# Requesting modulation weights two blocks in front of their sums in a two-layer hybrid trunk

## The chip, the cores and the metric

The kernel runs on one core of one Trainium2 chip. The metric is the device time of one execution in microseconds; the time quoted for a kernel is the median of its runs. The core's engines are called by the profile's names: PE (TensorE, matrix products), DVE (VectorE), ACT (ScalarE), POOL (GpSimd) and SP (SyncE, which here only issues transfers).

## The reference

Two layers run one after the other over x, 1024 positions by 1024 columns in float32. Each layer is conditioned by a vector c: three rows of 1024 numbers (shift, scale and gate) come from one product of SiLU(c) with a matrix of 1024 by 3072.

```python
c_act = jax.nn.silu(c)
...
mod = c_act @ w_mod + b_mod
shift, scale, gate = jnp.split(mod[:, None, :], 3, axis=-1)
h = rms_norm(x, pre_gain) * (1.0 + scale) + shift
proj = h @ w_in
...
y = jnp.concatenate([a_out, r_out, g_out], axis=-1) @ w_out
return x + gate * rms_norm(y, post_gain)
```

Between proj and y three groups of heads work on slices of proj: softmax attention over a window of 128 positions, retention, and gated linear attention (GLA), each multiplied by a SiLU gate of its own. The shift and the scale of a layer are needed before its input projection; its gate is needed only at its very end.

## The kernel before

**Tiling.** The positions are eight tiles of 128, the 1024 input columns eight blocks k of 128 (KT = 8). The big products run in float32 split into a high and a low part, in three passes on PE. The weights are cut into units of 256 columns (named gg, rg, rq, rk, rv, gqk, gv, kv, aq0, aq1, ag0, ag1 and o0 to o3). A unit comes in four transfers (`load`, its `issue` and `conv`): each lands in a staging tile, ACT (L157) or DVE (L159) copies the high part out of it into a large array, arena, and DVE or POOL subtracts to get the low part (L577).

**Staging tiles.** `stage()` gives a tile st of 128 by 512 floats. There are five of them (BST = 5), used in turn; a transfer into a tile waits until the last reader of what lay there before is done. Weight quarters, modulation weights and two small rows of gains all go through these five. The loader of the weights has up to three quarters in flight (LAG = 2).

**The modulation sums.** `mod_third(l, j)` computes one third of mod for layer l: j = 0 shift, 1 scale, 2 gate. A third is two halves (hh) of 512 columns, and a half is eight blocks k. Its inner `part(hh, k)` takes a staging tile and asks for the block's 128 by 512 numbers of w_mod (the transfer "lwm"). DVE multiplies each tile by the column k of c_act and adds it to the accumulator acc (L389 for the first block where j < 2, L391 for all others). At the end of a half PE sums acc over the partitions. The first layer's shift and scale are computed by another path, with tiles wm. So four thirds run through this code: the gate of layer 0, then scale and shift of layer 1, both begun in layer 0, and the gate of layer 1. Each has 16 tiles, 64 in all.

**What sets the order.** The program is written as generators, the jobs: a planner keeps a clock (`clk`) that counts PE's work, and `pump()` resumes each job when its planned delay (`yield lat("mod2", l)`, from the table L: 4.8 us in layer 0, 4.0 us in layer 1) is over. PE's instructions then run in just the order in which they were written. On DVE, ACT, POOL and SP a scheduler orders the instructions, with its own estimates, from the dependences and the order of writing. All transfers into staging tiles are issued by SP, one after the other; while SP waits for a tile to come free, everything behind it in its queue waits too.

In the kernel before, `mod_third` keeps a list `wts` of requested tiles: a block's sum takes the tile requested one block earlier, and the next block's request goes out in the same step. So at most two of the five staging tiles hold w_mod: the one being summed and the next.

**Names in the rows.** acc is the accumulator of a third; mx, t, sm, gs and mid are work tiles of the branches (gs a GLA tile of decay factors); smx holds attention weights; aux and mm are accumulators of PE; mixS, srS, sgS and aoS are arrays in the chip's memory through which branch outputs pass and come back. L1370 and L1380 are a GLA chunk's products, L1242 and L1246 the norm of a retention or GLA output, L1185 the softmax's reciprocal, L1073 a step of the rotation.

Of the kernel before, what the change touches and what calls it, by code (L numbers as in the profile page):

```python
# [23 lines left out]
KT = D // P  # L24
# [69 lines left out]
def trunk(ctx: ExitStack, tc: tile.TileContext, ins, cst, out):  # L94
# [21 lines left out]
    def nm(s):  # L116
        uid[0] += 1
        return f"{s}_{uid[0]}"
# [7 lines left out]
    def stage():  # L126
        return gp.tile([P, 512], F32, tag="st", name=nm("st"), bufs=BST)
# [7 lines left out]
    def aux(dt=F32):  # L135
        return ps.tile([P, 512], dt, tag="aux", name=nm("aux"), bufs=8 - MMB)
# [24 lines left out]
    def dma(k, dst, src):  # L161
        i = {"S": nc.sync, "A": A, "P": G}[EN[k]].dma_start(dst, src)
        if k in ("ssg", "ssr", "lsr", "lsg", "smh"):
            mark[2] = i
# [10 lines left out]
    def mult(dst, lhsT, rhs, start, stop, cost=None):  # L175
        T.matmul(dst, lhsT, rhs, start=start, stop=stop)  # L176
        if cost is not None:
            clk[0] += cost
            return
        n = 1  # L180
        for d in rhs.shape[1:]:
            n *= d
        c = n / 2400.0
        if rhs.dtype == F32R:
            c = max(c, 0.107 if lhsT.shape[-1] > 64 else 0.055)
        else:
            c = max(4 * c, 0.21 if n > 2 else 0.03)
        clk[0] += c
# [5 lines left out]
    def lat(key, l):  # L194

        return L[key + "@1"] if l and key + "@1" in L else L[key]
# [4 lines left out]
    def flag(name, lat=0.0):  # L201
        flags[name] = clk[0] + lat
# [100 lines left out]
    def mod_rows(l, j, eng=nc.sync):  # L303
        rows = t1()[0:16, 0:P]
        eng.dma_start(rows[0:8, :], b_mod[l:l + 1, j * D:(j + 1) * D].rearrange("o (k p) -> (o k) p", p=P))
        eng.dma_start(rows[8:16, :], pre_g[l:l + 1, :].rearrange("o (k p) -> (o k) p", p=P))
        return rows

    def mod_rows_t(rows, pool=aux):
        pr = pool()  # L310
        transp(pr[:, 0:16], rows, ident[0:16, 0:16])
        rc = small(16)
        V.tensor_copy(rc, pr[:, 0:16])
        return rc

    def mod_cols(l, j, hh, pm, rc):
        res = modc[(l, j)]
        ks = slice(4 * hh, 4 * hh + 4)
        if j == 0:
            V.tensor_tensor(res[:, ks], pm[:, 0:4], rc[:, ks], ALU.add)  # L320
        else:
            col = small(4)
            V.tensor_tensor(col, pm[:, 0:4], rc[:, ks], ALU.add)
            V.scalar_tensor_tensor(res[:, ks], col, 1.0, rc[:, 8 + 4 * hh:12 + 4 * hh], ALU.add, ALU.mult)

    def mod_tile(l, j):
        modc[(l, j)] = cp.tile([P, KT], F32, name=nm(f"mod{j}"), tag=f"mod{j}")
# [27 lines left out]
    def mod_third(l, j):  # L355
        wv = w_mod[l].rearrange("(p k) n -> p k n", k=KT)
        if j < 2:
            mod_tile(l, j)
            rows = mod_rows(l, j)
            yield lat("mod1", l)  # L360
            rc = mod_rows_t(rows)
        else:
            res = cp.tile([P, D], F32, name=nm("modg"), tag="modg")
            modg[l] = res
        wts = []

        def part(hh, k):
            wt = stage()
            c0 = j * D + 512 * hh
            dma("lwm", wt, wv[:, k, c0:c0 + 512])  # L370
            return wt

        for hh in range(2):
            c0 = j * D + 512 * hh
            acc = gp.tile([P, 512], F32, tag="acc", name=nm("acc"), bufs=1)
            if j == 2:
                G.memset(acc, 0.0)
                nc.sync.dma_start(acc[0:1, :], b_mod[l:l + 1, c0:c0 + 512])
            for k in range(KT):
                if wts:  # L380
                    wt = wts.pop()
                else:
                    wt = part(hh, k)
                    yield lat("mod2", l)
                n = KT * hh + k + 1
                if n < 2 * KT:
                    wts.append(part(n // KT, n % KT))
                if k == 0 and j < 2:
                    V.tensor_scalar(acc, wt, c_act[:, k:k + 1], None, ALU.mult)  # L389
                else:  # L390
                    V.scalar_tensor_tensor(acc, wt, c_act[:, k:k + 1], acc, ALU.mult, ALU.add)  # L391
                if k < KT - 1:
                    yield lat("mod2", l)
            yield lat("mod3", l)
            pm = aux()
            if j < 2:
                for b in range(4):
                    mult(pm[:, b:b + 1], acc[:, b * P:(b + 1) * P], ones[:, 0:1], True, True)
                mod_cols(l, j, hh, pm, rc)
                if j == 0:  # L400
                    flag(("modh", l, hh), lat("mod4", l))
            else:
                mult(pm, allones, acc, True, True)
                gain = stage()
                nc.sync.dma_start(gain, post_g[l:l + 1, 512 * hh:512 * hh + 512].to_broadcast((P, 512)))
                V.tensor_tensor(res[:, 512 * hh:512 * hh + 512], pm, gain, ALU.mult)
            yield lat("mod5", l)
        flag(("mod", l, j), lat("mod6", l))

    def mod_all(l, js, after=None):  # L410
        if after is not None:
            yield (0.0, after)
        else:
            yield L["ms"]
        for j in js:
            yield from mod_third(l, j)
# [1641 lines left out]
```

## Time and profile before

| | us |
|---|---|
| median of 3 runs | 986.1 |
| lowest and highest run | 984.17, 991.72 |
| the profiled execution | 981.63 |
| its span, first to last instruction | 979.9 |
| mean granted clock of PE (share of full) | 0.985 |

The profile covers one execution, 4.5 us quicker than the median. Its span is what the timeline's times count from. In the profile's rows, busy time is counted for each engine alone; an engine's idle time stands in brackets ahead of the instruction that ended it, with the one it waited for. A clock below 1.00 in a slice means that PE was granted only part of its clock there. The transfers' view lists 64 requests of w_mod tiles and 96 of w_in tiles, 256 KB each.

### The profile page before, as it was taken

The page shows a single profiled execution, that of the slowest core. Times are in us where ns is not written, and L with a number is a line of the kernel's source. Part 1 is how long each engine was busy: PE and PEld are TensorE (multiplying, and loading weights), DVE is VectorE, ACT ScalarE, POOL GpSimd, SP SyncE. Part 2 cuts the span into 40 slices and gives each one's busy share as a digit, 9 for nine tenths or more (in the row PEclk, how much of TensorE's full clock was granted, in tenths as well). Part 3 has the DMA queues.
Part 4 walks back from the last instruction along what each step waited for, and adds up shares of the span by engine and source line. Part 5 has one row for each costly group of instructions (what it writes and reads, how often), then busy time and mean ns, then how long its engine had stood idle before and what let it go on. Part 6 is the DMA issues. An engine that isn't in the chain of part 4 may idle for free.

```text
span 979.9 us, 19345 instructions
## 1 busy us (share of the span) xinstructions
PE 953.8 (97%) x7133; PEld 833.6 (85%) x7133; DVE 676.6 (69%) x1627; ACT 409.8 (42%) x1121; POOL 216.6 (22%) x252
## 2 busy tenths in 40 slices
PE   6999999999999999999999999999999999999996
PEld 1799999889998877778889999998899887778885
DVE  3897768567766777746577497775556578665885
ACT  3875134323322565534455431133323258752431
POOL 1112001213220333331023010122232124550300
PEclk8999999989999999999999999999999999999999
DMA  9825324433145355777555583362133323379973
GB/s 317 305 73 175 122 77 122 138 120 120 56 131 152 100 169 152 218 217 266 181 172 180 191 262 111 109 194 80 45 94 109 105 57 112 116 207 290 306 253 125
DMA packets 133454, 155.04 MB, mean 158 GB/s; under 512 B 13760, under 2 KB 95468, under 8 KB 133360
## 3 DMA queue, kind: packets, MB, share of 16 engines
q1 hardware_dynamic: 128240, 145.30, 47.6%
q10 hardware_dynamic: 5120, 8.51, 2.3%
q8 instruction: 56, 0.92, 0.4%
q14 instruction: 38, 0.31, 0.1%
HBM read 111.30 MB, written 40.37 MB: 155 GB/s over the span
## 4 chain that ended last, share of the span: by engine, by line
PE 82%; DVE 7%; DMA 5%; ACT 3%; issue 2%; POOL 1%; SPq 1%; DVEq 0%; POOLq 0%; ACTq 0%
PE mm L176 62%; PE aux L176 16%; PE aux L191 4%; DMA wm<-in_w_mod_dram 2%; DMA st<-in_w_in_dram 1%; POOL sm L725 1%; DMA st<-in_w_mod_dram 1%; ACT t L781 1%; DVE arena L577 0%; DVE t L1371 0%; DVE sm L1242 0%; DMA mixS<-t 0%; DVE acc L391 0%; DVE mx L1380 0%; DMA su<-in_w_out_dram 0%
## 5 line engine op out<-in xcount | busy, mean ns | idle before, releaser
L176 PE MATMUL mm<-arena,arena 128*128 128x256 f32 (+2 forms) x2880 | 458.2, 315 | 1.1 <-DVE t L1267 0.9
L176 PEld LDWEIGHTS mm<-arena,arena 128*128 128x128 f32 x2880 | 398.8, 189 | 35.4 <-issue 2.1
L176 PE MATMUL mm<-arena,mx 128*128 128x512 f32 (+1 forms) x564 | 127.6, 383 | 0.0
L176 PE MATMUL mm<-arena 128*128 128x256 f32 (+2 forms) x768 | 126.9, 320 | 0.5 <-ACT arena L792 0.5
L176 PEld LDWEIGHTS mm<-arena 128*128 128x128 f32 x768 | 110.8, 195 | 12.0 <-issue 2.2
L176 PEld LDWEIGHTS mm<-arena,mx 128*128 128x128 f32 x564 | 101.9, 188 | 20.6 <-issue 0.4
L725 POOL TENSOR_TENSOR sm<-sm,mhalf 128x1 f32<-128x1 f32 (+1 forms) x48 | 49.4, 1031 | 265.8 <-DVE sm L724 256.3
L157 ACT ACTIVATE arena<-st 128x512 fp32r<-128x512 f32 x102 | 61.1, 627 | 62.3 <-DMA st<-in_w_in_dram 24.4
L577 POOL TENSOR_TENSOR arena<-st,arena 128x512 fp32r<-128x512 f32 x26 | 39.2, 1507 | 127.1 <-ACT arena L157 116.9
L157 ACT ACTIVATE t<-aux 128x512 f32<-128x512 f32 (+1 forms) x86 | 48.0, 593 | 44.7 <-PE aux L191 25.6
L577 DVE TENSOR_TENSOR arena<-st,arena 128x512 fp32r<-128x512 f32 x82 | 63.2, 790 | 2.9 <-ACT arena L157 1.7
L1186 POOL TENSOR_TENSOR smx<-smx,sm 128x512 f32<-128x512 f32 x32 | 35.2, 1099 | 134.1 <-DVE sm L1185 123.4
L1182 ACT ACTIVATE smx<-smx,sm 128x129 f32<-128x129 f32 x128 | 49.9, 393 | 14.5 <-DVE sm L1179 14.2
L391 DVE SCALAR_TENSOR_TENSOR acc<-st,c_act,acc 128x512 f32<-128x512 f32 x60 | 45.8, 763 | 11.3 <-DMA st<-in_w_mod_dram 10.7
L176 PEld LDWEIGHTS aux<-t,mx 32*128 32x128 f32 (+1 forms) x896 | 44.4, 195 | 7.2 <-issue 3.0
L176 PE MATMUL aux<-t,mx 32*128 32x32 f32 (+1 forms) x896 | 45.6, 280 | 3.0 <-DVE gs L1350 1.5
L781 ACT ACTIVATE t<-aux,mod,mod 128x128 f32<-128x128 f32 x72 | 27.2, 464 | 35.3 <-DVE t L1540 22.5
L157 ACT ACTIVATE t<-mm 128x256 f32<-128x256 f32 x40 | 15.0, 382 | 57.8 <-PE mm L176 57.7
L191 PE MATMUL aux<-c_ident,t 128*128 128x128 f32 (+1 forms) x228 | 34.4, 278 | 0.5 <-DVE t L1247 0.4
L1175 DVE COPY_PREDICATED smx<-c_curmask,aux 128x256 f32<-128x256 int32 x64 | 25.2, 447 | 9.5 <-ACT smx L157 8.3
L191 PEld LDWEIGHTS aux<-c_ident,t 128*128 128x128 f32 (+1 forms) x228 | 26.8, 143 | 5.6 <-issue 1.6
L1240 ACT ACTIVATE t<-aux 128x512 f32<-128x512 f32 x16 | 9.5, 595 | 51.0 <-PE aux L176 51.0
(240 smaller groups left out, 1380.5 us busy)
## 6 DMA issues: line engine op xcount, KB each, us to landing
st<-in_w_in_dram SPq DMA_DIRECT2D x96, 256.0 KB, 3.4
st<-in_w_mod_dram SPq DMA_DIRECT2D x64, 256.0 KB, 3.0
mixS<-t SPq DMA_DIRECT2D x48, 256.0 KB, 2.3
mx<-mixS SPq DMA_DIRECT2D x20, 512.0 KB, 5.8
st<-in_w_out_dram SPq DMA_DIRECT2D x28, 256.0 KB, 3.0
wm<-in_w_mod_dram SPq DMA_DIRECT2D x10, 512.0 KB, 5.0
t<-tabS SPq DMA_DIRECT2D x16, 256.0 KB, 2.6
aoS<-t SPq DMA_DIRECT2D x32, 128.0 KB, 4.1
```

Source lines behind the costliest of these rows:

```text
L157: A.activation(dst, src, AF.Copy)
L176: T.matmul(dst, lhsT, rhs, start=start, stop=stop)
L191: T.transpose(dst, src, idn)
L391: V.scalar_tensor_tensor(acc, wt, c_act[:, k:k + 1], acc, ALU.mult, ALU.add)
L577: e.tensor_tensor(lo, st, f(hi), ALU.subtract)
L725: G.tensor_tensor(r, r, mhalf[:, :w], ALU.pow)
L781: A.activation(hf[0][:, ks], x[:, ks], AF.Identity, scale=gain, bias=shift)
L1175: V.copy_predicated(sv, curmask.unsqueeze(1).to_broadcast((P, 2, P)), pv[:, :, n // P - 1, :])
L1182: A.activation(sm[:, h, :], sm[:, h, :], AF.Exp, bias=mx[:, h:h + 1], accum_out=sums[:, h:h + 1])
L1186: eng("pn").tensor_tensor(sm[:, :, 0:128], sm[:, :, 0:128], rs.unsqueeze(2).to_broadcast((P, 4, P)), ALU.mult)
L1240: A.activation(sq, po, AF.Square)
```

## The change

Only the loop over the blocks in `mod_third` changes. A third now requests its first two tiles at once before its first delay; each block takes the oldest requested tile and asks for the tile two blocks further on. So three of the five staging tiles hold w_mod while a third runs: one being summed and two requested.

```diff
             for k in range(KT):
-                if wts:
-                    wt = wts.pop()
-                else:
-                    wt = part(hh, k)
+                if not wts:
+                    wts.extend((part(0, 0), part(0, 1)))
                     yield lat("mod2", l)
-                n = KT * hh + k + 1
+                wt = wts.pop(0)
+                n = KT * hh + k + 2
                 if n < 2 * KT:
                     wts.append(part(n // KT, n % KT))
```

PE's order is the same, instruction by instruction; the numbers of instructions are the same on every engine. On DVE and SP the order shifts around the sums. In the rows below, st, acc, t and the like carry the number of the tile, which the change shifts by one or two; the lines of the changed kernel from L381 on are one lower (L390 is the L391 of before).

**DVE, around 198 to 204 us of the profile before**: layer 1's scale begins (acc_2716), and behind its first sums stand the GLA product L1370 and the reduction L1242. Before:

```order
L389 TENSOR_SCALAR acc_2716<-st_2717,c_act 128x512
L391 SCALAR_TENSOR_TENSOR acc_2716<-st_2796,c_act,acc_2716 128x512
L391 SCALAR_TENSOR_TENSOR acc_2716<-st_2848,c_act,acc_2716 128x512
L391 SCALAR_TENSOR_TENSOR acc_2716<-st_2931,c_act,acc_2716 128x512
L391 SCALAR_TENSOR_TENSOR acc_2716<-st_3033,c_act,acc_2716 128x512
L1370 TENSOR_TENSOR t_413_2600<-t_394_2460,t_308_1924 128x512
L1242 TENSOR_REDUCE sm_2585<-t_408_2583 128x8
L1371 TENSOR_TENSOR t_414_2601<-t_394_2460,t_309_1925 128x512
```

After:

```order
L388 TENSOR_SCALAR acc_2716<-st_2717,c_act 128x512
L390 SCALAR_TENSOR_TENSOR acc_2716<-st_2719,c_act,acc_2716 128x512
L390 SCALAR_TENSOR_TENSOR acc_2716<-st_2798,c_act,acc_2716 128x512
L390 SCALAR_TENSOR_TENSOR acc_2716<-st_2850,c_act,acc_2716 128x512
L390 SCALAR_TENSOR_TENSOR acc_2716<-st_2933,c_act,acc_2716 128x512
L390 SCALAR_TENSOR_TENSOR acc_2716<-st_3035,c_act,acc_2716 128x512
L1369 TENSOR_TENSOR t_413_2600<-t_394_2460,t_309_1926 128x512
L1241 TENSOR_REDUCE sm_2585<-t_408_2583 128x8
L1370 TENSOR_TENSOR t_414_2601<-t_394_2460,t_310_1927 128x512
```

The extra row is the second tile, st_2719; six sums now stand ahead of the L1370 of before, where there were five.

**SP at the same place**: the requests from the fourth w_mod tile on, mixed with mixS stores, the load of a retention gate (srS) and quarters of the weight gqk or gv (w_in). Before:

```order
L162 DMA st_2848<-in_w_mod_dram 128x512
L162 DMA st_2931<-in_w_mod_dram 128x512
L162 DMA mixS<-t_398_2476 128x2x256
L162 DMA mixS<-t_399_2477 128x2x256
L162 DMA st_3033<-in_w_mod_dram 128x512
L162 DMA t_407_2581<-srS 128x2x256
L162 DMA st_3047<-in_w_in_dram 128x2x256
L162 DMA st_3076<-in_w_in_dram 128x2x256
L162 DMA st_3091<-in_w_mod_dram 128x512
```

After:

```order
L162 DMA st_2798<-in_w_mod_dram 128x512
L162 DMA st_2850<-in_w_mod_dram 128x512
L162 DMA mixS<-t_398_2476 128x2x256
L162 DMA mixS<-t_399_2477 128x2x256
L162 DMA st_2933<-in_w_mod_dram 128x512
L162 DMA t_407_2581<-srS 128x2x256
L162 DMA st_3035<-in_w_mod_dram 128x512
L162 DMA st_3049<-in_w_in_dram 128x2x256
L162 DMA st_3078<-in_w_in_dram 128x2x256
L162 DMA st_3093<-in_w_mod_dram 128x512
```

The sixth sum's tile, st_3035, stands where the weight quarter st_3047 stood, directly behind the load from srS; the weight quarters are one place later.

**DVE, around 86 to 96 us**: the gate of layer 0 (acc_1186) is being summed; L577 and L159 (L576 and L159) convert quarters of the weights rk and rv. Before:

```order
L577 TENSOR_TENSOR arena_73<-st_1171,arena_73 128x512
L391 SCALAR_TENSOR_TENSOR acc_1186<-st_1189,c_act,acc_1186 128x512
L1267 SCALAR_TENSOR_TENSOR t_194_1181<-t_189_1143,mm_1112 128x256
L1267 SCALAR_TENSOR_TENSOR t_199_1194<-t_193_1176,mm_1145 128x256
L577 TENSOR_TENSOR arena_73<-st_1192,arena_73 128x512
L159 CAST arena_254<-st_1203 128x512
L577 TENSOR_TENSOR arena_254<-st_1203,arena_254 128x512
```

After:

```order
L576 TENSOR_TENSOR arena_73<-st_1171,arena_73 128x512
L390 SCALAR_TENSOR_TENSOR acc_1186<-st_1189,c_act,acc_1186 128x512
L390 SCALAR_TENSOR_TENSOR acc_1186<-st_1191,c_act,acc_1186 128x512
L1266 SCALAR_TENSOR_TENSOR t_194_1181<-t_189_1143,mm_1112 128x256
L1266 SCALAR_TENSOR_TENSOR t_200_1196<-t_193_1176,mm_1145 128x256
L576 TENSOR_TENSOR arena_73<-st_1194,arena_73 128x512
L159 CAST arena_254<-st_1205 128x512
L576 TENSOR_TENSOR arena_254<-st_1205,arena_254 128x512
```

A second sum (st_1191) now stands ahead of the two L1267 (L1266), and the conversions follow one row later.

**SP, around 226 to 268 us**: the four quarters of the weight aq1 (w_in), with stores and loads of the branches between them and the next w_mod tiles. Before:

```order
L162 DMA st_3472<-in_w_in_dram 128x2x256
L162 DMA st_3497<-in_w_in_dram 128x2x256
L162 DMA st_3519<-in_w_in_dram 128x2x256
L162 DMA st_3578<-in_w_in_dram 128x2x256
L162 DMA mixS<-t_484_3041 128x2x256
L162 DMA mixS<-t_485_3042 128x2x256
L162 DMA t_510_3183<-sgS 128x2x256
L162 DMA mixS<-t_536_3363 128x2x256
L162 DMA mixS<-t_537_3364 128x2x256
L162 DMA t_552_3474<-sgS 128x2x256
L162 DMA st_3704<-in_w_mod_dram 128x512
```

After:

```order
L162 DMA st_3474<-in_w_in_dram 128x2x256
L162 DMA st_3499<-in_w_in_dram 128x2x256
L162 DMA st_3521<-in_w_in_dram 128x2x256
L162 DMA mixS<-t_485_3043 128x2x256
L162 DMA mixS<-t_486_3044 128x2x256
L162 DMA t_511_3185<-sgS 128x2x256
L162 DMA mixS<-t_537_3365 128x2x256
L162 DMA mixS<-t_538_3366 128x2x256
L162 DMA t_553_3476<-sgS 128x2x256
L162 DMA st_3580<-in_w_in_dram 128x2x256
L162 DMA st_3706<-in_w_mod_dram 128x512
```

The last quarter, st_3578 before and st_3580 after, moves from directly behind the third to behind six stores and loads, next to the following w_mod tiles.

## Prediction

> **What bounds the kernel now.** I read the page's busy shares and slices first, then the chain that ended last, then TensorE's own waits.
>
> ```profile
> span 979.9 us, 19345 instructions
> PE 953.8 (97%) x7133; PEld 833.6 (85%) x7133; DVE 676.6 (69%) x1627; ACT 409.8 (42%) x1121; POOL 216.6 (22%) x252
> PE   6999999999999999999999999999999999999996
> PEclk8999999989999999999999999999999999999999
> PE 82%; DVE 7%; DMA 5%; ACT 3%; issue 2%; POOL 1%; SPq 1%; DVEq 0%; POOLq 0%; ACTq 0%
> ```
>
> PE is busy for 953.8 of 979.9 us. Only 26.1 us are idle, most of it in the first and the last slice, where the digits are 6. The chain agrees: 82% of it is PE. A change to transfers can gain only where PE waits for them, so the next view is PE's waits, whole causes and not shares:
>
> ```profile
> PE mm L176 <- DMA wm<-in_w_mod_dram: 5.1, 2, 4.1
> PE mm L176 <- DVE mhalf L288: 4.7, 1, 4.7
> PE aux L176 <- DVE gs L1350: 1.5, 1, 1.5
> PE aux L176 <- DVE mx L1405: 1.5, 2, 1.1
> PE mm L176 <- DVE t L1267: 0.9, 1, 0.9
> PE aux L191 <- POOL smx L1186: 0.7, 1, 0.7
> ```
>
> The first two belong to the start, where the first layer's shift and scale come through other tiles (wm) that the change leaves alone. The view's other six causes come to 0.5 us or less each. No cause in it is a tile st of w_mod, and none is a weight converted out of an st. What the change aims at is on VectorE, in the groups of the page:
>
> ```profile
> L391 DVE SCALAR_TENSOR_TENSOR acc<-st,c_act,acc 128x512 f32<-128x512 f32 x60 | 45.8, 763 | 11.3 <-DMA st<-in_w_mod_dram 10.7
> st<-in_w_in_dram SPq DMA_DIRECT2D x96, 256.0 KB, 3.4
> st<-in_w_mod_dram SPq DMA_DIRECT2D x64, 256.0 KB, 3.0
> ```
>
> The second and third row are from the page's list of requests; the last number is the median time to landing in us. The 60 later sums take 763 ns each, and DVE sat idle for 10.7 us ahead of them until a tile of w_mod had landed. The question is how much of these 10.7 us reaches PE. The two longest waits stand in these rows of DVE's timeline, and behind them are the rows of PE:
>
> ```profile
> 288.18 0.75 DVE L391 SCALAR_TENSOR_TENSOR acc<-st,c_act,acc 128x512 f32<-128x512 f32 x1 [2.97 <-DMA st<-in_w_mod_dram]
> ...
> 414.08 2.33 DVE L391 SCALAR_TENSOR_TENSOR acc<-st,c_act,acc 128x512 f32<-128x512 f32 x3 [3.92 <-DMA st<-in_w_mod_dram]
> 416.32 0.17 DVE L1185 RECIPROCAL sm<-sm 128x4 f32<-128x4 f32 x1
> ```
>
> ```profile
> 417.67 0.66 PE L191 MATMUL aux<-c_ident,smx 128*128 128x128 f32 x4 [0.70 <-POOL smx L1186]
> ```
>
> ```profile
> 200.00:212.00 12.00, 10.51 (x109) 9.30 (x108) 9.84 (x27) 4.15 (x9) 3.30 (x5) 1.00 0.45 141
> 212.00:223.00 11.00, 11.00 (x94) 9.99 (x92) 4.57 (x13) 2.47 (x11) 2.89 (x6) 0.53 0.28 91
> 280.00:300.00 20.00, 20.00 (x151) 18.52 (x150) 15.05 (x43) 5.71 (x16) 3.44 (x4) 1.00 0.58 175
> 400.00:420.00 20.00, 19.16 (x138) 14.35 (x133) 14.06 (x29) 10.56 (x38) 5.52 (x9) 1.00 0.88 271
> 700.00:704.00 4.00, 4.00 (x20) 2.72 (x16) 2.72 (x16) 2.25 (x8) 0.00 (x0) 0.57 0.02 4
> ```
>
> In 280 to 300 us, around the wait of 2.97 us, PE is busy for 20.00 of 20.00 us: that wait costs nothing. Behind the wait of 3.92 us the reciprocal at 416.32 is late, POOL's product after it too, and PE stands for 0.70 us at 417.67. So of the 10.7 us I see at most 0.70 on PE.
>
> **The change part by part.** Arithmetic and counts stay: 64 requests, 64 sums, the same matmuls in the same order. What moves is where a w_mod tile stands among the other requests in SP's queue, which weight tiles fall behind it, and where sums stand on DVE. SP issues as many requests as before, about half a microsecond each (0.94 for two, below), so a moved w_mod request holds what it passes by that much and by its own transfer.
>
> *The place at 198 to 210 us.* It is the one where DVE is on the path.
>
> ```profile
> 198.54 3.12 DVE L391 SCALAR_TENSOR_TENSOR acc<-st,c_act,acc 128x512 f32<-128x512 f32 x4
> 202.47 0.69 DVE L1370 TENSOR_TENSOR t<-t,t 128x512 f32<-128x512 f32 x1 [0.81 <-PE aux L176]
> 203.49 0.69 DVE L1242 TENSOR_REDUCE sm<-t 128x8 f32<-128x512 f32 x1 [0.33 <-ACT t L1240]
> ...
> 209.64 0.15 DVE L1350 TENSOR_TENSOR gs<-gs,t 128x2 f32<-128x2 f32 x1
> ```
>
> ```profile
> 209.86 1.38 PE L176 MATMUL aux<-t,mx 32*128 32x32 f32 x41 [1.50 <-DVE gs L1350]
> ```
>
> ```profile
> 198.76 0.94 SPq L162 DMA_DIRECT2D st<-in_w_in_dram  x2
> ```
>
> From 203.49 on no row of DVE up to the gs of 209.64 carries an idle time, and PE waits 1.50 us for that gs. In the new order a sixth sum stands ahead of L1370, and its tile takes SP's place of 198.76, where a weight tile stands now. With the median of 3.0 us it lands at 201.76, just after the fifth sum's end (198.54 + 3.12 = 201.66), and the sum ends at 202.52; L1370 would end at 203.21, before 203.49: no cost. But SP issues several tiles there in a row. For such a stretch there is this row of the transfers issued between 89 and 91 us:
>
> ```profile
> st<-in_w_in_dram SPq DMA_DIRECT2D x3, 256.0 KB, 4.0
> ```
>
> With 4.0 us the tile lands at 202.76, the sum ends at 203.52, L1370 at 204.21, and the chain is 0.72 us late. Bounds 0 and 0.7. A w_mod tile's median is 0.4 us under a w_in tile's, so I take 3.6: landing 202.36, sum until 203.12, L1370 until 203.81: **+0.3 us**, all of it PE's, as nothing stands between gs and PE's wait.
>
> *The place at 86 to 102 us.* One sum more stands at about 91.4, and the weight tiles behind it are asked for one place later.
>
> ```profile
> 90.65 0.75 DVE L391 SCALAR_TENSOR_TENSOR acc<-st,c_act,acc 128x512 f32<-128x512 f32 x1
> ...
> 93.53 1.56 DVE L159 CAST arena<-st 128x512 fp32r<-128x512 f32 x1 [0.87 <-DMA st<-in_w_in_dram]
> ...
> 101.17 0.28 DVE L1073 TENSOR_TENSOR tr<-mm,sincos 128x128 f32<-128x128 f32 x1
> ```
>
> ```profile
> 88.80 2.33 SPq L162 DMA_DIRECT2D st<-in_w_in_dram  x3
> ```
>
> ```profile
> 101.62 5.62 PE L176 MATMUL mm<-arena,arena 128*128 128x256 f32 x46
> ```
>
> The sum's 0.75 fits into DVE's 0.87 idle before the cast of 93.53. The cast's tile comes one place later, 2.33 / 3 = 0.78 us. DVE then runs nearly without a gap to the L1073 of 101.17, which ends at 101.45 and frees an accumulator that PE takes again at 101.62. So PE may lose 0.78 - 0.17 = 0.6 at most; at least 0, since the number of DVE's operations up to that L1073 is the same by then. I take the middle, **+0.3 us**.
>
> *The rest, one line each.* The last three tiles of the third that ends at 414 us stand behind the same mx loads in both orders, so the wait of 3.92 us and PE's 0.70 stay: 0. A w_mod tile newly stands ahead of a mixS store there, and holds that store until its own place is freed by a sum; I put that at 0, since PE has other matmuls until the store's readers come, with half a sum, 0.4, as the upper bound. The wait of 2.97 us at 288 goes, with nothing gained, since PE was busy there; DVE only comes to its next wait earlier. One quarter of a weight (the unit aq1) falls far behind:
>
> ```profile
> 235.97 3.58 SPq L162 DMA_DIRECT2D st<-in_w_in_dram  x3
> ...
> 266.25 2.06 SPq L162 DMA_DIRECT2D st<-in_w_mod_dram  x3
> ```
>
> ```profile
> 305.08 1.30 PE L176 MATMUL mm<-arena 128*128 128x512 f32 x5
> ```
>
> The third tile of the first row moves to where the second begins. Its conversions are these, the second on POOL:
>
> ```profile
> L157 ACT ACTIVATE arena<-st 128x512 fp32r<-128x512 f32 x102 | 61.1, 627 | 62.3 <-DMA st<-in_w_in_dram 24.4
> L577 POOL TENSOR_TENSOR arena<-st,arena 128x512 fp32r<-128x512 f32 x26 | 39.2, 1507 | 127.1 <-ACT arena L157 116.9
> ```
>
> It is ready at 266.25 + 3.4 + 0.63 + 1.51 = 271.8, and PE's first matmul with that unit is the one of 305.08: 33 us of cover, cost 0.
>
> Sum: 0.3 + 0.3 = +0.6 us; bounds by these rows -0.7 (PE's stall at 417.67 gone) and +1.7. The profiled execution took 981.63 us, 4.5 us under the median of 986.1; by the median the forecast is 986.7.
>
> *What the clock adds.* In 212 to 223 us PE's granted clock is 0.53: (1 - 0.53) x 11.00 = 5.2 us lost, right behind the wait of 1.50 us. In 700 to 704 it is 0.57: 1.7 us. So a changed wait at 209 can move more than itself. [...]
>
> **The rivals.**
> Faster: the 10.7 us come back whole, because DVE, relieved of its waits, delivers everything earlier. For it speaks only their size; against it PE's 20.00 of 20.00 us around the longest but one. It would give 986.1 - 10.7 = 975.4. [...]
> Clock: the wait at 209 grows and the half-clock stretch with it, or another of the short ones comes up (+1.7 to +5.2 on the sum: 988.4 to 991.9); or the wait falls elsewhere and the stretch doesn't come (986.7 - 5.2 = 981.5).
> Slower: three of the five tiles are w_mod's, so only two are left to the weights. The quarter of aq1 decides it: if PE needed it when it lies now, the loss would run up to 266.25 - 239.55 = 26.7 us (239.55 is the end of SP's row that begins at 235.97), 986.1 + 26.7 = 1012.8. The turning point is 271.8, the end of its conversion; PE's first use is at 305.08, and no PE wait today is for a weight.
> No effect: SP issues as far ahead as tiles come free, whatever the program's depth, so the requests land when they landed. For it speaks that at 198.76 SP's place is taken right after DVE's first sum has freed a tile, in both orders, only for another tile. Against it: which tile it is decides what lands. It gives 986.1.
>
> **How the numbers follow.** Forecast, a small cost near 986.7: 0.57. No effect: 0.16. Clock up 0.10, clock down 0.07, faster 0.04, slower 0.06. Changes of 1% (9.9 us) are about what a measurement of this kernel can tell from none. Faster by over 1% is the first rival alone, which ends at -1.1%: 0.04. Slower by over 1%: 0.06. Within: 0.90. The range takes in the clock both ways: 981.5 to 992, which leaves out only the faster and the slower rival.
>
> **What would show it.** Right: DVE's wait at 288 gone and that at 414 kept, PE's wait for gs L1350 at 1.5 to 2.2 us, PE busy for 953 to 955 us. Wrong: a PE wait on arena or st that isn't there now (weights late), the gs wait shorter (the sixth sum hidden), or PEclk below 9 in another slice than the ninth.

## The result, and the profile after

| | before | changed |
|---|---|---|
| median, us (16 runs each) | 986.03 | 990.86 |
| lowest and highest | 981.9, 991.72 | 986.14, 997.96 |
| ratio | | 1.006, interval 1.004 to 1.008 |
| the profiled execution, us | 981.63 | 997.96 |

The changed kernel is 4.8 us slower by the medians: inside the forecast's range and within 1%, but eight times the +0.6 us that the sum had given. The profiled execution is the longest of the 16, so its own difference of 16 us is not the change's. Of the twelve executions of a later run of the changed kernel, two took 1176.81 and 1873.90 us in a slower state and are left out of its figures.

The head of the page of the changed kernel, with the row of the sums and, from the list of transfers, the median landing time:

```profile
span 996.1 us, 19343 instructions
PE 965.4 (97%) x7133; PEld 843.2 (85%) x7133; DVE 678.7 (68%) x1627; ACT 411.3 (41%) x1121; POOL 217.0 (22%) x252
PEclk9999999979979999999999999999799999999999
L390 DVE SCALAR_TENSOR_TENSOR acc<-st,c_act,acc 128x512 f32<-128x512 f32 x60 | 47.1, 785 | 8.0 <-DMA st<-in_w_mod_dram 7.5
st<-in_w_mod_dram SPq DMA_DIRECT2D x64, 256.0 KB, 3.1
```

What the change aims at happened: DVE's idle time ahead of the sums fell from 10.7 to 7.5 us. It bought nothing. PE's work rose by 11.6 us at the same number of instructions, so it ran more of them at a low clock: the mean granted clock is 0.973 here and 0.985 before, and three slices carry a 7, where before only one stood at 8 after the first. PE's waits (engine, line, cause, us in total, times, longest):

```profile
PE aux L176 <- DVE gs L1349: 2.3, 1, 2.3
PE mm L176 <- ACT arena L791: 1.6, 1, 1.6
PE aux L176 <- DVE mx L1404: 1.5, 2, 1.1
PE aux L191 <- DVE mx L1379: 1.4, 2, 0.9
PE mm L176 <- DVE t L1266: 1.1, 1, 1.1
PE aux L176 <- DVE stR L1490: 0.9, 1, 0.9
PE aux L176 <- DVE t L1245: 0.8, 1, 0.8
PE aux L176 <- DVE t L1465: 0.7, 1, 0.7
```

The wait for gs grew from 1.5 to 2.3 us, and three causes of over half a microsecond are new: L1245 (0.8), L1490 (0.9) and L1465 (0.7). POOL's smx (0.7) is gone. The arena of L791 (1.6 us, 0.5 before) is not a weight but the high part of the layer's modulated input, and PE waits for it at 51 us, before the first changed sum (91.6 us). No cause is a weight.

**The first place.** DVE's timeline of the changed kernel (start, us, engine, line, operation, idle ahead of it), then POOL's, SP's and PE's:

```profile
199.54 3.11 DVE L390 SCALAR_TENSOR_TENSOR acc<-st,c_act,acc 128x512 f32<-128x512 f32 x4
203.75 0.75 DVE L390 SCALAR_TENSOR_TENSOR acc<-st,c_act,acc 128x512 f32<-128x512 f32 x1 [1.10 <-DMA st<-in_w_mod_dram]
204.42 0.69 DVE L1369 TENSOR_TENSOR t<-t,t 128x512 f32<-128x512 f32 x1
205.03 0.68 DVE L1241 TENSOR_REDUCE sm<-t 128x8 f32<-128x512 f32 x1
205.62 0.78 DVE L1370 TENSOR_TENSOR t<-t,t 128x512 f32<-128x512 f32 x1
206.32 0.58 DVE L723 TENSOR_SCALAR sm<-sm 128x8 f32<-128x8 f32 x1
...
210.83 0.68 DVE L1245 TENSOR_TENSOR t<-aux,sm 128x512 f32<-128x512 f32 x1
211.43 0.15 DVE L1349 TENSOR_TENSOR gs<-gs,t 128x2 f32<-128x2 f32 x1
```

```profile
205.81 1.07 POOL L1382 TENSOR_TENSOR t<-t,gs 128x256 f32<-128x256 f32 x1
```

```profile
199.76 0.42 SPq L162 DMA_DIRECT2D st<-in_w_mod_dram  x1
```

```profile
211.65 2.52 PE L176 MATMUL aux<-t,mx 32*128 32x32 f32 x41 [2.28 <-DVE gs L1349]
```

The sixth sum's tile was asked for at 199.76 and the sum could begin at 203.75: 4.0 us, not the 3.6 that I took. DVE stood idle for 1.10 us ahead of it, and L1369 followed without a wait of its own. From there the order is that of before, but not every duration is. Before, DVE and POOL had these rows:

```profile
204.09 0.93 DVE L1371 TENSOR_TENSOR t<-t,t 128x512 f32<-128x512 f32 x1
204.95 0.16 DVE L724 TENSOR_SCALAR sm<-sm 128x8 f32<-128x8 f32 x1
```

```profile
203.86 0.62 POOL L1383 TENSOR_TENSOR t<-t,gs 128x256 f32<-128x256 f32 x1
```

The matmuls of PE ahead of this place run 1.0 us later in the profile of the changed kernel. Counted from them, L1241 is 0.5 us late (205.03 against 203.49 + 1.0) and gs 0.8 us (211.43 against 209.64 + 1.0). The late sum is thus 0.5 us of it. The other 0.3 us arise beside POOL: L723 now lies beside L1382 and takes 0.58 instead of 0.16 us, while L1370 takes 0.78 instead of 0.93. PE's wait is 0.78 us longer.

The profile puts this wait down to gs, but in the built program PE waits there for L1245 (L1246 of before). That instruction reads out the accumulator aux that PE's next product is to fill. It ends at 211.51, and gs, behind it, at 211.58, so the two can hardly be told apart by time. The name gs is kept below.

**The second place** is not in the prediction. DVE, POOL and PE of the changed kernel around 273 us:

```profile
268.67 1.90 DVE L576 TENSOR_TENSOR arena<-st,arena 128x512 fp32r<-128x512 f32 x3 [0.52 <-PE mm L176]
...
273.00 1.19 DVE L723 TENSOR_SCALAR sm<-sm 128x8 f32<-128x8 f32 x1
275.94 0.69 DVE L1245 TENSOR_TENSOR t<-aux,sm 128x512 f32<-128x512 f32 x1 [1.75 <-POOL sm L724]
```

```profile
272.87 1.30 POOL L576 TENSOR_TENSOR arena<-st,arena 128x512 fp32r<-128x512 f32 x1 [0.69 <-ACT arena L157]
274.27 1.64 POOL L724 TENSOR_TENSOR sm<-sm,mhalf 128x8 f32<-128x8 f32 x1
```

```profile
276.78 1.38 PE L176 MATMUL aux<-t,mx 32*128 32x32 f32 x41 [0.80 <-DVE t L1245]
```

And the same work before:

```profile
265.53 2.97 DVE L577 TENSOR_TENSOR arena<-st,arena 128x512 fp32r<-128x512 f32 x3 [0.52 <-PE mm L176]
...
269.86 0.17 DVE L724 TENSOR_SCALAR sm<-sm 128x8 f32<-128x8 f32 x1
```

```profile
266.57 1.38 POOL L577 TENSOR_TENSOR arena<-st,arena 128x512 fp32r<-128x512 f32 x1 [3.41 <-ACT arena L157]
```

POOL's subtraction is that of the last aq1 quarter. What DVE did beside it took about 1 us longer in both kernels. Before, that was the three subtractions of the other quarters (2.97 us, against 1.90 without POOL beside them), behind which PE had no wait. Now the quarter is converted some 3 us later against that work, and what it lies beside is the L723 of 8 columns, 1.19 instead of 0.17 us. L723 feeds POOL's L724, L724 feeds DVE's L1245, and for L1245, which again reads out an accumulator, PE waits 0.80 us.

**The clock.** Windows of the changed kernel (the third number from the end is PE's granted clock):

```profile
200.00:212.00 12.00, 9.72 (x73) 8.60 (x72) 10.79 (x28) 2.75 (x5) 3.74 (x5) 0.96 0.55 173
212.00:225.00 13.00, 13.00 (x133) 11.77 (x130) 4.66 (x14) 4.37 (x16) 1.33 (x3) 0.51 0.18 53
270.00:279.00 9.00, 8.20 (x112) 7.70 (x111) 5.45 (x14) 2.55 (x8) 3.50 (x4) 1.00 0.41 118
279.00:290.00 11.00, 11.00 (x97) 10.71 (x96) 4.85 (x19) 1.74 (x8) 0.96 (x2) 0.53 0.08 25
```

Behind the new wait at 276 us stand 11 us at a clock of 0.53 (5.2 us lost), where the execution of before had 1.00 in 272 to 290 us. Which stretches carry such a low clock differs between the profiles, also where the waits are alike (behind a wait of 0.51 us for mx, 0.57 and then 1.00 in 700 to 704 and 704 to 708 us of before, 0.61 and then 0.50 in 712 to 716 and 716 to 720 us here; more figures below), so this row shows a possibility, not a price.

### The profile page after: what moved, and what is told of

It is laid out like the page before. It is cut to its first block, busy times and chain, and to the rows that moved or that the text cites. A ratio compares the mean times of both kernels' runs of the same rounds, so it can differ in the third digit from the quotient of the medians.

```text
span 996.1 us, 19343 instructions
## 1 busy us (share of the span) xinstructions
PE 965.4 (97%) x7133; PEld 843.2 (85%) x7133; DVE 678.7 (68%) x1627; ACT 411.3 (41%) x1121; POOL 217.0 (22%) x252
## 4 chain that ended last, share of the span: by engine, by line
PE 77%; DVE 9%; DMA 7%; ACT 3%; issue 2%; POOL 1%; SPq 0%; DVEq 0%; POOLq 0%; ACTq 0%
PE mm L176 57%; PE aux L176 16%; PE aux L191 4%; DMA su<-in_w_out_dram 1%; DMA st<-in_w_in_dram 1%; DMA wm<-in_w_mod_dram 1%; POOL sm L724 1%; DMA st<-in_w_mod_dram 1%; ACT t L780 1%; DMA xk<-in_x_dram 1%; DVE arena L576 0%; DVE sm L1241 0%; DMA twS<-su 0%; DVE t L353 0%; DVE t L1370 0%
## 5 line engine op out<-in xcount | busy, mean ns | idle before, releaser
L176 PE MATMUL mm<-arena,arena 128*128 128x256 f32 (+2 forms) x2880 | 464.0, 317 | 1.3 <-DVE t L1266 1.1
L176 PEld LDWEIGHTS mm<-arena,arena 128*128 128x128 f32 x2880 | 403.6, 191 | 36.2 <-issue 2.1
L724 POOL TENSOR_TENSOR sm<-sm,mhalf 128x1 f32<-128x1 f32 (+1 forms) x48 | 49.0, 1021 | 265.6 <-DVE sm L723 265.3
L576 POOL TENSOR_TENSOR arena<-st,arena 128x512 fp32r<-128x512 f32 x26 | 39.3, 1511 | 125.9 <-ACT arena L157 125.9
L576 DVE TENSOR_TENSOR arena<-st,arena 128x512 fp32r<-128x512 f32 x82 | 61.4, 767 | 5.5 <-ACT arena L157 4.4
L176 PEld LDWEIGHTS aux<-t,mx 32*128 32x128 f32 (+1 forms) x896 | 48.1, 216 | 9.2 <-issue 4.5
L176 PE MATMUL aux<-t,mx 32*128 32x32 f32 (+1 forms) x896 | 49.5, 299 | 4.6 <-DVE gs L1349 2.3
L390 DVE SCALAR_TENSOR_TENSOR acc<-st,c_act,acc 128x512 f32<-128x512 f32 x60 | 47.1, 785 | 8.0 <-DMA st<-in_w_mod_dram 7.5
```

The lines of the kernel that those rows point to most:

```text
L576: e.tensor_tensor(lo, st, f(hi), ALU.subtract)
L724: G.tensor_tensor(r, r, mhalf[:, :w], ALU.pow)
```

## The experiments

The loop was rewritten so that the number of blocks requested ahead can depend on the third and the block; PE's order is that of before in all of these kernels.

### One third at a time

```diff
-                if not wts:
-                    wts.extend((part(0, 0), part(0, 1)))
+                two = (l, j) == (1, 1)
+                if not wts:
+                    wts.extend(part(0, i) for i in range(2 if two else 1))
...
-                n = KT * hh + k + 2
+                n = KT * hh + k + (2 if two else 1)
```

The condition is (1, 1) for layer 1's scale, (0, 2) for layer 0's gate, (1, 0) for layer 1's shift, (1, 2) for layer 1's gate.

> Two blocks ahead in one of the four thirds alone, layer 1's scale; the others as before. Theory A (two collisions in this third: the sixth sum ahead of the GLA chain at 204 us, and the last aq1 quarter, whose POOL subtraction then lies beside a short DVE instruction at 273 us): most of the loss is here, +3 to +5 us on the median, PE's wait for gs near 2.3 us, a new PE wait of 0.8 to 1.1 us at 276 us with half-clock behind it. Theory B (weights late because three of five tiles are held, in every third alike): about +1.2 us. Theory C (only the clock's chance): within 1.5 us of before, and no new PE wait.

> Two blocks ahead in layer 0's gate alone (86 to 196 us). Theory A: no new PE wait, within 1 us of before; the stall of up to 0.6 us that the prediction allowed at 101.6 us doesn't come. Theory B: about +1.2 us. Theory C: within 1.5 us.

> Two blocks ahead in layer 1's shift alone (279 to 430 us). Theory A: no new PE wait of over 0.3 us; PE's 0.7 us at 417 us may go; -1 to +0.5 us. Theory B: about +1.2 us. Theory C: within 1.5 us.

> Two blocks ahead in layer 1's gate alone (560 to 690 us). Theory A: the two PE waits that the changed kernel has at 602 and 610 us (0.7 and 0.9 us, behind late su and twS transfers) come here too, and no others: +1 to +2 us. Theory B: about +1.2 us, as weights late. Theory C: within 1.5 us, and those two waits are not in this profile, as they would be a chance of one execution.

Measured on one chip, beside a median of 986.34 us for the kernel before:

| two ahead only in | median, us | ratio and interval |
|---|---|---|
| layer 1's scale | 991.81 | 1.0052 (1.0026 to 1.0079) |
| layer 0's gate | 986.12 | 1.0007 (0.9990 to 1.0024) |
| layer 1's shift | 985.86 | 0.9998 (0.9979 to 1.0016) |
| layer 1's gate | 985.23 | 0.9992 (0.9973 to 1.0011) |

The whole loss is in layer 1's scale. Its rows show both places again, PE's waits first, then DVE:

```profile
PE aux L176 <- DVE gs L1350: 2.3, 1, 2.3
...
PE aux L176 <- DVE t L1246: 0.8, 1, 0.8
```

```profile
272.62 1.18 DVE L724 TENSOR_SCALAR sm<-sm 128x8 f32<-128x8 f32 x1
```

Theory B (each third costs the same, as weights come late) falls. Theory A's guess for layer 1's gate falls too: the waits of 0.9 and 0.7 us at 610 and 602 us came in that kernel only as 0.2 and 0.4, without a loss. Waits for the same two lines, of 0.2 to 0.7 us at 597 to 604 us, stand also in kernels below that leave this third as it was, so I count them as chance of one execution. PE's wait for smx at 417 us is no part of the change either: it was gone from the changed kernel's profile, 1.3 us in the one with the scale alone, and absent from the one with layer 0's gate alone.

### The two places apart

In layer 1's scale the second block ahead was limited to some of the 16 blocks:

```diff
+                d = 2 if (l, j) == (1, 1) and KT * hh + k < 7 else 1
...
+                while nx < 2 * KT and len(wts) < d:
+                    wts.append(part(nx // KT, nx % KT))
+                    nx += 1
```

With `< 7` the order has the sixth sum at 204 us and the aq1 quarter where it was. With `>= 7` it is the other way round. With `hh == 1` it has neither, with `hh == 0` both.

> Layer 1's scale, two blocks ahead only for the first seven blocks of its first half: the sixth sum stands ahead of the GLA chain at 204 us, the aq1 quarter stays where it was. Theory A1 (the sixth sum's wait for its tile delays the chain): PE's wait for gs 2.2 to 2.4 us instead of 1.5, none at 276 us, the median 1 to 3 us up. Theory A2 (only the aq1 quarter matters): gs wait up as well, but the median within 0.7 us of before.

> Layer 1's scale, two blocks ahead only from the eighth block of its first half on: no sixth sum at 204 us, but the last aq1 quarter behind the six stores and loads, with its POOL subtraction beside the reduction's L724 at 272 us. Theory A2 (the late quarter's conversion collides): gs wait 1.5 us, a new PE wait of 0.8 to 1.1 us at 276 us, L724 over 1 us long there instead of 0.17, the median 1 to 4 us up. Theory A1: the median within 0.7 us of before, as the clock makes the rest.

> Layer 1's scale, two blocks ahead only in its second half: neither the sixth sum at 204 us nor the late aq1 quarter. Theories A1 and A2: no new PE wait of over 0.3 us up to 300 us, within 1 us of before. Rival (any second block ahead in this third costs): 2 us or more.

> Layer 1's scale, two blocks ahead in its first half: the sixth sum and the late aq1 quarter together. Theory A: both waits (gs 2.2 to 2.8 us, and 0.8 to 1.1 us at 275 us), 1.5 to 2.5 us of PE's time and 2 to 6 us over before with the clock. If the parts only add up as measured apart (0.0 and 0.14%): 1.5 us or less.

| two ahead in | gs wait, us | wait near 275 us | ratio and interval |
|---|---|---|---|
| blocks 0 to 6 (sixth sum) | 2.8 | none | 1.0000 (0.9975 to 1.0026) |
| blocks 7 to 15 (quarter) | 1.5 | 0.7 | 1.0014 (0.9992 to 1.0035) |
| the second half (neither) | 1.5 | none | 1.0000 (0.9973 to 1.0026) |
| the first half (both) | 1.7 | 0.8 | 1.0020 (0.9995 to 1.0045) |

Each wait comes with its own cause and goes with it. With the sixth sum alone, DVE's rows:

```profile
204.36 0.75 DVE L392 SCALAR_TENSOR_TENSOR acc<-st,c_act,acc 128x512 f32<-128x512 f32 x1 [1.35 <-DMA st<-in_w_mod_dram]
...
206.92 0.58 DVE L725 TENSOR_SCALAR sm<-sm 128x8 f32<-128x8 f32 x1
```

With both, the wait for gs was 1.7 us and not the 2.2 to 2.8 expected. DVE's rows there:

```profile
203.47 0.75 DVE L392 SCALAR_TENSOR_TENSOR acc<-st,c_act,acc 128x512 f32<-128x512 f32 x1 [0.49 <-DMA st<-in_w_mod_dram]
...
204.82 0.69 DVE L1243 TENSOR_REDUCE sm<-t 128x8 f32<-128x512 f32 x1
...
206.03 0.58 DVE L725 TENSOR_SCALAR sm<-sm 128x8 f32<-128x8 f32 x1
```

PE's matmuls run 1.3 us later here than before, so L1243 is on time (203.49 + 1.3): in this execution the sixth sum's tile cost nothing, and the 0.2 us come from L725, which took 0.58 us here too, where it took 0.16 before.

With the quarter alone, DVE, POOL and PE:

```profile
271.71 1.14 DVE L725 TENSOR_SCALAR sm<-sm 128x8 f32<-128x8 f32 x1
```

```profile
271.53 1.29 POOL L578 TENSOR_TENSOR arena<-st,arena 128x512 fp32r<-128x512 f32 x1 [0.64 <-ACT arena L157]
```

```profile
275.44 1.38 PE L176 MATMUL aux<-t,mx 32*128 32x32 f32 x41 [0.75 <-DVE t L1247]
```

But the times of the parts don't reach the scale's 0.52%: both intervals of the single places hold 1, and so does that of the two together. The interval of the two together also overlaps that of the scale, so the gap itself is not clear of the scatter. A wait of 0.8 us is 0.08%, under what these runs can tell: by the medians the quarter alone is 2.7 us over before, within A2's 1 to 4, but the second half alone, with neither wait, is 1.0 us over. A1 had expected 1 to 3 us for the sixth sum, with a gs wait of 2.2 to 2.4 us; its interval ends at +2.6. So the wait at each place is shown, its price in the median is not.

### Undoing it, and the change again

> The change in three thirds, undone in layer 1's scale. Theory A (both places are in that third): gs wait 1.5 us, no wait at 276 us, within 1.5 us of before. Theory B (every third costs): 3 us or more over before.

> The changed kernel once more, beside the next three on one chip. If the 0.6% is the kernel's and not the chip's or the hour's, 3 to 7 us over before, with the gs wait at 2.2 to 2.4 us and a wait of 0.8 to 1.1 us at 276 us; the waits of 0.7 and 0.9 us at 602 and 610 us of the first profile may or may not be there.

On one chip, beside 986.95 us for before: the change without layer 1's scale (`two = (l, j) != (1, 1)`) took 985.88 us, ratio 1.0001 (0.9978 to 1.0025). The whole change took 989.97 us, the median of its ten executions, ratio 1.0036 (1.0009 to 1.0063): 3.0 us over before by the medians, within the 3 to 7 expected. Its profile is that of the 1176.81 us at a granted clock of 0.743, where PE waits for wm and mhalf alone; so the two waits that were expected are not confirmed by it, though L723 took 0.94 us beside POOL's L576 there too. PE's wait for gs without the scale:

```profile
PE aux L176 <- DVE gs L1350: 1.5, 1, 1.5
```

With the change undone in that third alone the loss is gone, and gs is back at 1.5. Nothing is won by the other three thirds either: DVE's shorter waits there reach nobody.

### Six staging tiles, and a longer chain

```diff
-B2, B1, BS, BST, MMB, SMB = 10, 8, 13, 5, 3, 4
+B2, B1, BS, BST, MMB, SMB = 10, 8, 13, 6, 3, 4
...
-CPAD, GPAD, APAD = 480, 192, 192
+CPAD, GPAD, APAD = 448, 192, 192
```

> The kernel before, one block ahead, with six staging tiles instead of five. The sixth tile lets the scheduler put one more sum ahead of the GLA chain at 204 us as well. Theory A1: gs wait 2.0 to 2.4 us and the median 1 to 3 us up, though only one block is requested ahead. Rival D (the weights starve because three of five tiles are held): gs wait 1.5 us, the median within 1 us of before or under it.

One block ahead and six tiles: 988.51 us beside 987.70, ratio 1.0005 (0.9982 to 1.0027). A1's expectation missed. The sixth sum did come and did wait, even longer:

```profile
207.12 0.75 DVE L391 SCALAR_TENSOR_TENSOR acc<-st,c_act,acc 128x512 f32<-128x512 f32 x1 [2.11 <-DMA st<-in_w_mod_dram]
```

Yet PE had no wait for gs; its longest stop nearby was 1.20 us for L1405 at 217 us. DVE's order behind the sum is that of the changed kernel, up to L1246 (214.20 to 214.87) and gs. But in this program the accumulator that L1246 reads out goes to a later instruction of PE, a small transpose at 214.92, which waits 0.20 us. So it shows that a second block ahead isn't needed for the sixth sum, and that the sum alone doesn't set PE's wait: which instruction of PE takes the freed accumulator does too. Rival D's time came true, within 1 us of before, though not its gs wait of 1.5 us.

```diff
-        V.tensor_tensor(a1, qk, dA, ALU.mult)
+        for _ in range(5 if (l, p) == (0, 0) else 1):
+            V.tensor_tensor(a1, qk, dA, ALU.mult)
```

> The kernel before, with the GLA product L1370 of the chain at 203 us computed five times over instead of once (the same result each time): four DVE instructions of about 0.6 us more ahead of the gs that PE waits for. If a delay of this chain costs what it lasts: PE's wait there 3.5 to 4 us and 2.4 us over before. If the clock multiplies it: the half-clock stretch behind it 13.7 us or longer and 4 us or more over before. If PE has room there: less than 1 us.

987.48 us beside 986.95, ratio 1.0002 (0.9975 to 1.0029). It didn't test what it was built for: the scheduler spread the repeated products among the chain's other instructions and moved the gs steps ahead. In place of PE's wait of 1.5 us for gs stand three:

```profile
209.45 0.44 PE L191 MATMUL aux<-c_ident,mx 128*128 128x128 f32 x2 [0.92 <-DVE mx L1381]
210.07 1.69 PE L176 MATMUL aux<-t,mx 32*128 32x32 f32 x47 [0.19 <-POOL mx L1381]
...
214.25 0.23 PE L191 MATMUL aux<-c_ident,t 16*128 16x16 f32 x1 [1.02 <-DVE t L1246]
```

Together they are 2.1 us, 0.6 more than before, for 2.4 us of added DVE work. The 47 matmuls at 210.07 begin before the gs that the wait had been put down to (L1350, here at 211.26): they don't need it. The accumulator that L1246 reads out goes to the transpose at 214.25, as with six tiles. How the clock answers to a longer wait stays open.

### How much is the clock

Each run gives its span and mean granted clock. Span x (1 - clock) is what a PE that is always busy would lose; span x clock is the rest. Means over the runs of each kernel, in us, beside runs of before taken together with them (about 35 each; the first row is set beside those of the second):

| kernel | lost to the clock | the rest | rest of before |
|---|---|---|---|
| changed (16 runs) | 21.8 | 968.2 | 964.7 |
| layer 1's scale alone | 21.1 | 967.8 | 964.7 |
| changed again (10 runs) | 21.5 | 967.1 | 965.1 |
| first half | 21.2 | 966.2 | 965.1 |
| quarter alone | 20.8 | 967.2 | 966.5 |
| sixth sum alone | 19.7 | 967.0 | 966.5 |
| second half alone | 22.1 | 964.8 | 966.5 |
| without the scale | 20.0 | 965.0 | 965.1 |

Before loses 19.7, 19.6 and 19.7 us in its three groups of runs. The standard error of a mean is 0.5 to 1.2 us for the clock's part and 0.3 to 0.8 us for the rest. The rest grows by 2.0 to 3.5 us in the kernels with the whole scale, and by 1.1, 0.7 and 0.5 us with both places in the first half and with each alone, about the size of the waits in the profiles, but within two standard errors of nothing. The clock takes about 2 us more in the changed kernel. But the second half alone, whose ratio is 1.0000, has the largest clock loss of all; so the clock's share is a tendency of these runs and not shown to come from the two waits. The profiles say the same: with the gs wait at 1.5 us each time, PE's clock in 209 to 225 us was 0.68 before, 1.00 with layer 1's shift alone and 0.89 with layer 1's gate alone; and in 272 to 290 us it was 0.91 in both of these, which have no wait there, as with the quarter alone, which has one.

## Why the prediction was right or wrong

The measured time is inside the range, but the sum gave +0.6 us, an eighth of the 4.8 that came. The range reached that far because of the clock, of whose part only a tendency is shown; so the hit is in good part luck.

- **That nothing is gained**: right, for the reason given. DVE's waits for w_mod fell by 3.2 us and PE didn't notice. One reading on the way was wrong: of the view's other causes, one was over 0.5 us, PE's wait for mx of L1380 with 1.4 us in two waits. It is 1.4 in the changed kernel too (L1379).
- **The +0.3 us at 198 to 210 us** is a term that was mis-sized. The late sum came as described: sixth sum, late tile, L1370 behind it. I took 3.6 us for the tile between bounds of 3.0 and 4.0; the upper bound is what came, and the chain was 0.5 us late by it. A part that the prediction lacked made it 0.8, over the bound of 0.7: a short DVE instruction of the chain came to lie beside POOL. In two other kernels the wait grew by 0.2 and 1.3 us, so it varies: DVE's idle time ahead of the sixth sum was 0.49 and 1.35 us there. And it was not gs itself that PE needed, but the accumulator that the instruction ahead of gs reads out.
- **The +0.3 us at 86 to 102 us**: didn't come; the lower bound, 0, did. The cast came 0.8 us late, as forecast (95.29, with PE's matmuls 0.97 us later, against 93.53), but one sum fewer stood behind it, and the rotation's step that frees the accumulator was on time. With that third alone there is no such wait either, and the median is 0.2 us under before.
- **"33 us of cover, cost 0" for the aq1 quarter** is the step that failed. The cover was right as far as it went: the weight was never late. But I asked only when its data are needed, and not what its conversion lies beside. Its POOL subtraction moved beside a short DVE instruction on the path and cost PE 0.8 us. In the trace POOL's L576 ran from 272.87 to 274.17 and DVE's L723, which began behind it, from 273.00 to 274.19: 1.19 us, and an end 0.02 us behind the subtraction's. In the kernels with the scale alone, with the quarter alone and with the first half alone the same instruction took 1.18, 1.14 and 1.24 us and ended 0.03 us behind POOL's subtraction each time. Why it takes longer there, no run shows.
- **PE's 0.70 us at 417 us "stay"**: neither right nor wrong; it is there in some profiles and not in others.
- **The clock** was in the range, not in the sum. The changed kernel lost about 2 us more to it, with a standard error of over 1 us; the step of 5.2 us behind one wait, the rival's price, was seen in one execution and isn't the mean.
- **The rivals**: weights starving, the slower one, is refuted: no PE wait is for a weight in any of these profiles. Faster didn't come. "No effect" holds for three of the four thirds. "Clock up", at 988.4 to 991.9, has the measured time inside; the runs show about 2 us more lost to the clock, but not that the longer wait at 209 us brought it.
- **The signs**: DVE's wait of 2.97 us at 288 us is gone; that of 3.92 us at 414 us is kept in part (2.54 us, at 421.71). The other signs of being right missed: the gs wait is 2.28 us, over 2.2, and PE is busy for 965.4 us. Of the signs of being wrong one came, PEclk below 9 outside the ninth slice: it is 7 in the twelfth and the twenty-ninth too.

The sum corrected by what was measured is 0.8 + 0.8 = 1.6 us of waits. The two measurements of the whole change gave 4.8 and 3.0 us by the medians. About 2 us of that stands beside a larger clock loss; the 1 us or so that remains in the first is open, and so is whether the two places together, in the first half alone, really cost less (0.2%, with an interval up to 0.45%).

## What to carry to other kernels

Asking earlier for data helps only where the engine that bounds the kernel waits for them; here DVE waited, 10.7 us before and 7.5 after, and PE did not. More tiles in flight let a scheduler pull work forward, and the instruction pulled forward can stand, waiting for its own data (1.10 us here), ahead of one that is ready. When a transfer moves, follow its consumers too: what they run beside can matter more than when the data are needed (here 1.19 instead of 0.17 us for L723, with the weight never late). And where a profile names the instruction that ended a wait, see what ended just ahead of it: here PE waited for an accumulator to be read out.

## What the runs showed of the hardware

A DVE instruction on 8 columns took 1.14 to 1.24 us in four kernels beside a POOL subtraction of 1.29 or 1.30 us, 0.58 us beside a shorter overlap (0.56 us) with another POOL instruction, and 0.16 or 0.17 us without one; three large ones took 2.97 us beside a POOL subtraction of 1.38 us and 1.90 us without one. The granted clock differs between executions of one kernel: over the 16 runs of the changed kernel it lay between 0.968 and 0.986, and the time between 986.14 and 997.96 us.
